# First query block of a hybrid encoder step: the products with x's low part put last, and a fixed VectorE order in the prologue

## The chip, the cores and the metric

The kernel runs on one core of a Trainium2 chip. The metric is the time of one execution in microseconds (us) on the device, as the median of several. Smaller is better. Engines are TensorE (PE; PEld its weight loads), VectorE (DVE), ScalarE (ACT), GpSimd (POOL) and SyncE (SP), whose queue issues all transfers.

## The reference

One inference step of a one-layer encoder. x (1024 prompt and 128 sample tokens, 1024 wide) is projected by one matrix into the queries, keys and values of three groups of heads and into a gate. The heads are band attention (A), differential attention (B) and attention to 256 memory tokens (M), whose keys and values are projected from `mem`.

```python
h = jnp.einsum('bsd,de->bse', x, w_in)
a_q, a_k, a_v, b_q, b_k, b_v, m_q, gate = jnp.split(h, PROJ_SPLITS, axis=-1)
mk, mv = memory_kv(mem_prompt, w_mem_kv[layer])
o_a = band_attention_prompt(aq, ak, av, a_rel_bias[layer])
o_b = diff_post(diff_attention_prompt(bq, bk, bv, lam), diff_subln_g[layer], lambda_init)
o_m = memory_attention(mq, mk, mv)
y = jnp.einsum('bse,ed->bsd', mixed * jax.nn.silu(gate), w_out)
return layer_norm(DEEPNORM_ALPHA * x + y, g, b)
```

## The kernel before

Every product is made of three passes over numbers that are split into a high part and a low part: high by high, low by high, high by low (`step`, L141 to L144). The high part is a cast on ScalarE into a shorter format; the low part is the number less its high part, a subtraction (`tensor_tensor`) with two inputs in SBUF, on VectorE or GpSimd.

**The prologue** (L192 to L278) does the following. `load_mem_w` (L202) loads and splits the weights of four memory blocks (two of keys, two of values) and, with block 0, `mem`; some subtractions are VectorE's, the rest GpSimd's. `load_next` (L129) loads and splits the weights of the next block of the projection; their low parts are GpSimd's. `load_x` (L222) loads a chunk c of x: x is cut into three chunks of 384 tokens (`CH`), each loaded in four pieces of two k-tiles, twelve pieces in all. ScalarE casts every piece (L199); the low parts (L200) of the odd pieces are VectorE's, those of the even pieces GpSimd's (`XP`). The pieces go through six buffers (`xr`), so that from the seventh on a piece's transfer waits until an earlier piece has been split. `mem_part` (L245) makes a memory block: 24 products of 256 columns (`mem_block`), a copy out of PSUM on VectorE (L236), and for the values (blocks 2 and 3) two transposes and a copy on ScalarE. `split_mem` (L178) splits the first unit's keys (`split_k`, L163: four casts on ScalarE, L167 and L168, two VectorE subtractions, L169) and its values (L183, L184). The tiles of the weights of blocks 2 and 3 (`ka`, `va`) are taken over by the split keys and values.

**The first query block** (L1117 to L1120) projects x into the queries of memory unit M0: for each chunk, `chunk` (L316) emits eight k-steps of the three passes, 24 products of 384 columns, and then `evac`: `split_q` (L147) takes the chunk out of PSUM in two halves, each a ScalarE activation (L155) and a VectorE subtraction (L159) with one input in PSUM. The products go into PSUM tiles `pp`, of which there are two; a chunk therefore waits until the chunk two places before it has been evacuated. Behind the query block come B0's keys (`k_block`) and the attention of M0, whose scores (L444, L445) need the split queries and keys.

**What sets the order.** A list scheduler places the instructions of each engine by priority and by its own estimate of when operands are ready; `manual_schedule(engines={...})` keeps the program's order for the engines named. Before, that held for SP in the prologue and for TensorE within one k-step. Each engine then runs its list strictly in order.

Of the kernel before, what the change touches and what calls it, by code (L numbers as in the profile page):

```python
# [7 lines left out]
F32 = mybir.dt.float32  # L8
# [7 lines left out]
P = 128  # L16
KT = 8
NTOK = 1152
NPR = 1024
CH = 384  # L20
# [2 lines left out]
EPS = 1e-5  # L23
BIG = 1e30
SP_ = 100
HP = 300
RR = 0.98
RL = 0.95
# [8 lines left out]
XP = [2, 6]  # L37
# [4 lines left out]
NG = [0, 1, 1, 1, 1, 1, 1, 2]  # L42
GW = 2
PE = mybir.EngineType.PE
SP = mybir.EngineType.SP
GATES = [2, 3, 4, 5, 0, 1, 6, 7]
SWAP = [i ^ 1 for i in range(32)]
# [15 lines left out]
def hybrid_step(tc, d, o):  # L63
    nc = tc.nc
# [11 lines left out]
    ps_p = pool("ps_p", 2, space=PSUM)  # L76
# [36 lines left out]
    names = [(n[0], int(n[1])) for n in ORD]  # L113
    base = {"A": (0, 2, 4), "B": (6, 10, 14), "M": (18,)}
    order = [base[names[0][0]][0] + names[0][1]]
    gates = iter(GATES)
# [5 lines left out]
    loaded = {}  # L122
# [6 lines left out]
    def load_next(early=None):  # L129
        if len(loaded) == len(order):  # L130
            return
        blk = order[len(loaded)]
        hi = wst.tile([P, KT, P], F32R, tag="whi")
        lo = wst.tile([P, KT, P], F32R, tag="wlo")
        loaded[blk] = (hi, lo)
        for i in range(2):
            raw = early.tile([P, 4, P], F32, tag="mraw", bufs=MB) if early else wst.tile([P, 4, P], F32, tag="wraw")
            nc.sync.dma_start(raw, d["win"][blk, :, 512 * i : 512 * i + 512].rearrange("p (k c) -> p k c", c=P))
            split_half(hi, lo, raw, i, nc.gpsimd)
# [32 lines left out]
    def setup(kind, idx):  # L172
        u = Unit()
        u.kind, u.idx = kind, idx
        u.slot = {"A": 0, "B": 2, "M": 6}[kind] + idx
        u.sqz = sqzs[ORD.index(kind + str(idx)) % 2]
        return u

    def split_mem(u, kv, v):
        u.ka = [op_.tile([P, 256], F32R, tag=f"ka{i}") for i in range(2)]  # L180
        split_k(kv, 256, u.ka, kl, 0)
        u.va = op_.tile([P, 2, 2, P], F32R, tag="va")
        nc.scalar.copy(u.va[:, :, :, 0:64], v)  # L183
        nc.vector.tensor_tensor(out=u.va[:, :, :, 64:128], in0=v, in1=f(u.va[:, :, :, 0:64]), op=ALU.subtract)  # L184
# [7 lines left out]
    with tc.tile_pool(name="early", bufs=1) as ep_:  # L192
        ep = Pool(ep_)
        memh = ep.tile([P, KT, 256], F32R, tag="memh")
        meml = ep.tile([P, KT, 256], F32R, tag="meml")
        wm = []

        def split_part(hi, lo, raw, a, b, eng):
            nc.scalar.copy(hi[:, a:b], raw)  # L199
            eng.tensor_tensor(out=lo[:, a:b], in0=raw, in1=f(hi[:, a:b]), op=ALU.subtract)  # L200

        def load_mem_w(blk):  # L202
            if blk < 2:
                hi, lo = [op_.tile([P, KT, P], F32R, tag=f"qa{i}", bufs=2) for i in range(2)]
            else:
                if blk == 2:
                    hi, lo = [op_.tile([P, KT, P], F32R, tag=f"ka{i}") for i in range(2)]
                else:
                    both = op_.tile([P, 2, KT, P], F32R, tag="va")
                    hi, lo = both[:, 0], both[:, 1]  # L210
            wm.append((hi, lo))
            cut = PC if blk == 0 else [0, 4, 8]
            for i, (a, b) in enumerate(zip(cut, cut[1:])):
                raw = ep.tile([P, b - a, P], F32, tag="mraw", bufs=MB)
                nc.sync.dma_start(raw, d["wmem"][blk, :, P * a : P * b].rearrange("p (k c) -> p k c", c=P))
                split_part(hi, lo, raw, a, b, nc.gpsimd if i or blk == 0 else nc.vector)
                if blk == 0:
                    memr = ep.tile([P, b - a, 256], F32, tag="xr", bufs=XB)
                    nc.sync.dma_start(memr, d["memT"][:, 256 * a : 256 * b].rearrange("p (k c) -> p k c", c=256))
                    split_part(memh, meml, memr, a, b, nc.vector)  # L220

        def load_x(c):  # L222
            for a in range(0, KT, 2):
                xr = ep.tile([P, 2, CH], F32, tag="xr", bufs=XB)
                nc.sync.dma_start(xr, d["xT"][c, :, CH * a : CH * (a + 2)].rearrange("p (k c) -> p k c", c=CH))
                split_part(xh[c], xl[c], xr, a, a + 2, nc.gpsimd if a in XP else nc.vector)

        kvs = []

        def mem_block(blk):  # L230
            ps = ps_p.tile([P, 256], F32, tag="pp")
            for k in range(KT):
                step(ps, wm[blk], memh, meml, k)
            kv = ep.tile([P, 256], F32, tag=f"memkv{blk}")
            kvs.append(kv)
            nc.vector.tensor_copy(kv, ps)  # L236


        warm = ps_t.tile([P, P], F32, tag="pt")
        for _ in range(WU):  # L240
            nc.tensor.matmul(warm, lhsT=sqzs[0][0], rhs=sqzs[0][0], start=True, stop=True)
        stores = []
        mem0 = []

        def mem_part(blk):  # L245
            mem_block(blk)
            out, scr = (o["mkT"], mkscr) if blk < 2 else (o["mvT"], mvscr)
            stores.append((out[blk % 2], kvs[blk]))
            if blk == 1:
                stores.append((mkscr, kvs[blk]))  # L250
            if blk < 2:
                return
            pt = ps_t.tile([P, 2, P], F32, tag="pt")
            for t in range(2):
                nc.tensor.transpose(pt[:, t], kvs[blk][:, t * P : (t + 1) * P], ident)
            mv = ep.tile([P, 2, P], F32, tag=f"memv{blk}")
            nc.scalar.copy(mv, pt)
            if blk == 3:
                stores.append((mvscr.rearrange("p (t e) -> p t e", t=2), mv))
            else:  # L260
                mem0.append(mv)

        with tc.manual_schedule(engines={SP}):
            for blk in range(4):
                load_mem_w(blk)
            load_next(ep)
            load_x(0)
            for blk in range(4):
                mem_part(blk)
            load_x(1)  # L270
            load_x(2)
            load_next()
            for out, kv in stores:
                nc.sync.dma_start(out, kv)
            nc.sync.dma_start(cos, d["cos"])
            nc.sync.dma_start(sin, d["sin"])
        units = [setup(*n) for n in names]
        split_mem(units[0], kvs[0], mem0[0].rearrange("p t (h e) -> p t h e", h=2))  # L278

    tmp = pool("tmp", 2)  # L280
    pp = pool("pp", 6)
# [56 lines left out]
    def project(blk, evac):  # L338
        return [chunk(blk, c, evac, c == 0) for c in range(3)]
# [9 lines left out]
        nc.vector.tensor_tensor(out=t1, in0=t1, in1=t2, op=ALU.add)  # L349
        return t1  # L350

    def q_block(u, blk, scale):
        def evac(c, ps):
            if c == 0:
                u.qa = [op_.tile([P, NPR], F32R, tag=f"qa{i}", bufs=2) for i in range(2)]
            n = npr(c)
            if u.kind == "B":
                src, sc = rope(ps, c, scale), 1.0
            else:
                src, sc = ps, scale  # L360
            split_q(src, sc, n, u.qa, c * CH)
            if c == 2:
                for m in range(2):
                    r = slice(64 * m, 64 * m + 64)
                    nc.scalar.activation(u.sqz[m][r], src[r, n:CH], AF.Copy, scale=sc)

        return project(blk, evac)

    def k_block(u, blk, out, skip):
        def evac(c, ps):  # L370
# [54 lines left out]
    def gate_block(slot):  # L425


        def evac(c, ps):
            t = tmp.tile([P, CH], F32, tag="t1", bufs=3)
            nc.scalar.activation(t, ps, AF.Tanh, scale=0.5)  # L430
            nc.vector.scalar_tensor_tensor(out=t, in0=t, scalar=1.0, in1=ps, op0=ALU.add, op1=ALU.mult)
            nc.sync.dma_start(
                gscr[3 * c : 3 * c + 3, :, slot].rearrange("t p c -> p t c"), t.rearrange("p (t c) -> p t c", c=P))

        return project(20 + slot, evac)
# [493 lines left out]
    def emit(items):  # L929
        for x in items:  # L930
            x[1]()
# [24 lines left out]
    def q_of(u):  # L956
        return q_block(u, base[u.kind][0] + u.idx, -0.125 if u.kind == "A" else 0.125)

    def k_of(u):
        if u.kind == "M":  # L960
            if u is not units[0]:
                load_mem(u)
            return []
        if u.kind == "B":
            return k_block(u, 10 + u.idx, o["bkT"][u.idx], 0)
        return k_block(u, 2 + u.idx, o["akT"][u.idx], 512)
# [147 lines left out]

    stages = []
    late = []
    first = [q_of(units[0])] + [gate_block(next(gates)) for _ in range(NG[0])]  # L1117
    for parts in zip(*first):
        for part in parts:
            emit(part)  # L1120
    for i, u in enumerate(units):
        nxt = units[i + 1] if i + 1 < len(units) else None
        emit(with_stages(sum(k_of(u), []), EV))
# [139 lines left out]
```

## Time and profile before

| what | value |
|---|---|
| runs | 685.92, 685.08, 683.6 us |
| median | 685.08 us |
| profiled execution | 685.8 us, its span 684.0 us |
| TensorE busy | 662.8 us (97%) |
| VectorE busy | 472.6 us (69%) |
| ScalarE busy | 356.3 us (52%) |
| GpSimd busy | 233.5 us (34%) |

The times of the profile count from the start of the span. A matmul's duration in the rows is its latency; matmuls overlap, so two in a row start closer together than they last. A row of the timeline merges equal neighbours (x2, x3) and ends, where the engine had been idle, with that idle time and what ended it.

### The profile page before, as it was taken

Reading aid. Unit: us, or ns where it says so; the run is one execution under the profiler, and the core shown is the slowest. Engines: PE = TensorE matmul, PEld = TensorE weight load, DVE = VectorE, ACT = ScalarE, POOL = GpSimd, SP = SyncE. Lnnn points to the kernel's source line nnn. Section 1 sums busy time; section 2 is a strip of 40 time slices with the busy share of each in tenths; the row PEclk is TensorE's granted clock in tenths of the full one; section 3 lists DMA queues with packets and bytes.
Section 4 is the critical chain, followed back from the end, with each engine's and each line's share of the span. In section 5 each row is a group of like instructions: output and inputs, shape, how many; then the busy total and the mean of one; then the engine's idle time right before and its main releaser. Section 6 shows DMA issues by size and latency. Waiting matters only on the chain. (4 is left out here: it accounts for less than half of the span.)

```text
span 684.0 us, 12210 instructions
## 1 busy us (share of the span) xinstructions
PE 662.8 (97%) x4306; PEld 614.2 (90%) x4306; DVE 472.6 (69%) x1169; ACT 356.3 (52%) x922; POOL 233.5 (34%) x282
## 2 busy tenths in 40 slices
PE   8899999999999999999999999999999996999995
PEld 7789999999999999999999999999999985787884
DVE  4869966796579856897566435673666678677854
ACT  5748845566446645565456535764566684111000
POOL 7654212632344224532323433323133231324102
PEclk9999999999999999999999999999999998899999
DMA  8761432121312222142302132233222648684411
GB/s 276 247 218 45 150 130 74 39 87 54 97 58 78 82 86 74 41 165 83 87 29 78 59 90 63 78 104 103 84 82 89 206 135 305 219 285 156 154 61 62
DMA packets 55694, 78.91 MB, mean 115 GB/s; under 512 B 9369, under 2 KB 33233, under 8 KB 55633
## 3 DMA queue, kind: packets, MB, share of 16 engines
q1 hardware_dynamic: 55632, 78.13, 34.6%
q8 instruction: 34, 0.56, 0.3%
q14 instruction: 28, 0.22, 0.1%
HBM read 57.69 MB, written 20.42 MB: 114 GB/s over the span
## 5 line engine op out<-in xcount | busy, mean ns | idle before, releaser
L143 PE MATMUL pp<-xl,whi 128*128 128x384 f32 x672 | 229.1, 341 | 2.6 <-DVE xl L200 1.8
L142 PE MATMUL pp<-xh,whi 128*128 128x384 f32 x672 | 230.5, 343 | 0.3 <-DVE qa L159 0.2
L144 PE MATMUL pp<-xh,wlo 128*128 128x384 f32 x672 | 228.9, 341 | 0.0
L143 PEld LDWEIGHTS pp<-xl,whi 128*128 128x128 f32 x672 | 126.6, 188 | 5.8 <-DVE xl L200 2.4
L142 PEld LDWEIGHTS pp<-xh,whi 128*128 128x128 f32 x672 | 126.4, 188 | 3.4 <-issue 0.7
L144 PEld LDWEIGHTS pp<-xh,wlo 128*128 128x128 f32 x672 | 126.4, 188 | 1.7 <-issue 0.2
L127 POOL TENSOR_TENSOR wlo<-wraw,whi 128x512 fp32r<-128x512 f32 x54 | 72.4, 1361 | 66.1 <-ACT whi L126 50.9
L586 ACT ACTIVATE p<-ps,nm 128x512 f32<-128x512 f32 (+3 forms) x96 | 55.2, 580 | 47.8 <-DVE nm L583 36.2
L444 PE MATMUL ps<-ka,qa 128*128 128x512 f32 (+4 forms) x176 | 58.5, 338 | 0.5 <-DVE nm L693 0.5
L445 PE MATMUL ps<-kl,qa 128*128 128x512 f32 (+4 forms) x176 | 57.3, 328 | 0.0
L457 PE MATMUL pt<-ident,p 128*128 128x128 f32 x332 | 55.0, 274 | 0.7 <-DVE p L526 0.6
L581 DVE TENSOR_REDUCE nm<-ps 128x1 f32<-128x512 f32 (+3 forms) x96 | 51.0, 549 | 1.6
L461 DVE TENSOR_TENSOR ptl<-pt,pth 128x512 fp32r<-128x512 f32 x56 | 38.2, 684 | 12.2 <-ACT pth L460 11.7
L457 PEld LDWEIGHTS pt<-ident,p 128*128 128x128 f32 x332 | 39.6, 141 | 4.4 <-DVE p L526 0.8
L701 POOL TENSOR_SCALAR p<-p,rs 128x640 f32<-128x640 f32 (+4 forms) x32 | 21.5, 676 | 64.3 <-DVE rs L700 58.7
L460 ACT CAST pth<-pt 128x512 fp32r<-128x512 f32 x56 | 32.6, 588 | 20.9 <-PE pt L457 19.9
L1028 PE MATMUL pp<-xh,whi 128*128 128x512 f32 (+1 forms) x96 | 37.5, 392 | 4.5 <-ACT whi L992 4.5
L1028 PE MATMUL pp<-xh,wlo 128*128 128x512 f32 (+1 forms) x96 | 37.0, 387 | 1.4 <-DVE rs L1051 1.4
L1028 PE MATMUL pp<-xl,whi 128*128 128x512 f32 (+1 forms) x96 | 37.1, 386 | 0.0
L992 ACT CAST whi<-p 128x1024 fp32r<-128x1024 f32 (+2 forms) x9 | 8.6, 954 | 53.5 <-PE pp L1028 42.9
L465 DVE TENSOR_TENSOR ptl<-pt,pth 128x256 fp32r<-128x256 f32 (+1 forms) x72 | 25.2, 352 | 15.8 <-ACT pth L464 15.2
L620 PE MATMUL po<-pth,va 128*128 128x256 f32 (+1 forms) x160 | 35.4, 285 | 0.0
(225 smaller groups left out, 1352.9 us busy)
## 6 DMA issues: line engine op xcount, KB each, us to landing
wraw<-in_win SPq DMA_DIRECT2D x54, 256.0 KB, 3.2
xr<-in_xT SPq DMA_DIRECT2D x12, 384.0 KB, 4.0
gates<-t SPq DMA_DIRECT2D x24, 192.0 KB, 2.2
qa<-in_xn SPq DMA_DIRECT2D x9, 512.0 KB, 5.0
wraw<-in_wout SPq DMA_DIRECT2D x16, 256.0 KB, 2.6
p<-gates SPq DMA_DIRECT2D x8, 512.0 KB
out_y<-qa SPq DMA_DIRECT2D x16, 256.0 KB, 2.3
mixed<-od SPq DMA_DIRECT2D x28, 128.0 KB, 1.8
```

The costliest lines, as they stand in the source:

```text
L127: eng.tensor_tensor(out=lo[:, h], in0=raw, in1=f(hi[:, h]), op=ALU.subtract)
L142: nc.tensor.matmul(ps, lhsT=w[0][:, k], rhs=xh_[:, k], start=(k == 0), stop=False)
L143: nc.tensor.matmul(ps, lhsT=w[0][:, k], rhs=xl_[:, k], start=False, stop=False)
L144: nc.tensor.matmul(ps, lhsT=w[1][:, k], rhs=xh_[:, k], start=False, stop=(k == KT - 1))
L444: nc.tensor.matmul(ps, lhsT=u.qa[h][:, qs], rhs=u.ka[h][:, k0 : k0 + n], start=True, stop=False)
L445: nc.tensor.matmul(ps, lhsT=u.qa[h][:, qs], rhs=kl[h][:, k0 : k0 + n], start=False, stop=True)
L457: nc.tensor.transpose(pt[:, t, q * P : (q + 1) * P], p[q][:, cols[t][q] : cols[t][q] + P], ident)
L461: nc.vector.tensor_tensor(out=lo, in0=pt, in1=f(hi), op=ALU.subtract)
L581: nc.vector.tensor_reduce(out=nm[:, m, c : c + 1], in_=ps[c][:, : b - a], axis=AX.X, op=ALU.max, negate=True)
L586: nc.scalar.activation(e[:, a:b], ps[c][:, : b - a], AF.Exp, bias=nm[:, m, 0:1], accum_out=rs[:, m, c : c + 1])
L620: nc.tensor.matmul(out, lhsT=a, rhs=b, start=(g == 0 and x == 0), stop=(g == j and x == len(mm) - 1))
L1028: nc.tensor.matmul(y, lhsT=a[:, k], rhs=b[k][:, s], start=(k == 0 and x == 0), stop=(k == KT - 1 and x == 2))
```

## The change

Three things are edited. First, `q_first` takes the place of the first query block's loop: for chunks 0 and 1, and then for chunk 2, it emits the 16 products with x's high part for each chunk, and after those the eight with x's low part, followed by the evacuation. Second, in the prologue VectorE is added to the engines that keep the program's order, and that program is written in another order: all weight splits, memory blocks 0 to 2, x's chunk 0, memory block 3, chunks 1 and 2, and only then `split_mem`. Third, the casts and subtractions of x get a higher priority (`XPR`).

```diff
@@ load_x
-                split_part(xh[c], xl[c], xr, a, a + 2, nc.gpsimd if a in XP else nc.vector)
+                with tc.high_priority(offset=XPR):
+                    split_part(xh[c], xl[c], xr, a, a + 2, nc.gpsimd if a in XP else nc.vector)
@@ prologue
-        with tc.manual_schedule(engines={SP}):
+        units = [setup(*n) for n in names]
+        with tc.manual_schedule(engines={SP, DVE}):
             for blk in range(4):
                 load_mem_w(blk)
             load_next(ep)
+            for blk in range(3):
+                mem_part(blk)
             load_x(0)
-            for blk in range(4):
-                mem_part(blk)
+            mem_part(3)
             load_x(1)
             load_x(2)
+            split_mem(units[0], kvs[0], mem0[0].rearrange("p t (h e) -> p t h e", h=2))
             load_next()
...
-        units = [setup(*n) for n in names]
-        split_mem(units[0], kvs[0], mem0[0].rearrange("p t (h e) -> p t h e", h=2))
@@ query block
+    def q_first(u):
+
+        evac = q_evac(u, 0.125)
+        blk = base[u.kind][0] + u.idx
+        for cs in ((0, 1), (2,)):
+            ps = {}
+            for low in range(2):
+                for c in cs:
+                    if not low:
+                        ps[c] = ps_p.tile([P, CH], F32, tag="pp")
+                        if c == 0:
+                            load_next()
+                    w = loaded[blk]
+                    with tc.manual_schedule(engines={PE}):
+                        for k in range(KT):
+                            if low:
+                                nc.tensor.matmul(ps[c], lhsT=w[0][:, k], rhs=xl[c][:, k], start=False, stop=(k == KT - 1))
+                            else:
+                                nc.tensor.matmul(ps[c], lhsT=w[0][:, k], rhs=xh[c][:, k], start=(k == 0), stop=False)
+                                nc.tensor.matmul(ps[c], lhsT=w[1][:, k], rhs=xh[c][:, k], start=False, stop=False)
+                    if low:
+                        with tc.high_priority(offset=HP):
+                            evac(c, ps[c])
...
-    first = [q_of(units[0])] + [gate_block(next(gates)) for _ in range(NG[0])]
-    for parts in zip(*first):
-        for part in parts:
-            emit(part)
+    q_first(units[0])
```

`q_evac` is the evacuation that `q_block` had, as a function of its own.

How VectorE's list reads where the memory part ends. Here `memkv` is the copy of a memory block, `qa`, `ka` and `va` on the left of L200 (L202) are low parts of memory weights. Before:

```order
L200 TENSOR_TENSOR qa_45_178<-mraw_179,qa_44_177 128x512
L236 COPY memkv_64_257<-pp_232 128x256
L200 TENSOR_TENSOR ka_49_188<-mraw_189,ka_48_187 128x512
L200 TENSOR_TENSOR va_197<-mraw_198,va_197 128x512
L299 TENSOR_SCALAR subg_92<-subg_92 128x1
L236 COPY memkv_66_284<-pp_259 128x256
```

Changed:

```order
L202 TENSOR_TENSOR qa_45_178<-mraw_179,qa_44_177 128x512
L202 TENSOR_TENSOR ka_49_188<-mraw_189,ka_48_187 128x512
L202 TENSOR_TENSOR va_197<-mraw_198,va_197 128x512
L239 COPY memkv_60_241<-pp_216 128x256
L303 TENSOR_SCALAR subg_92<-subg_92 128x1
L239 COPY memkv_62_268<-pp_243 128x256
```

The copy of block 0 moved behind the splits of the weights of blocks 2 and 3.

VectorE's list from there to the evacuation of chunk 1. `xl` is x's low part, `kl` that of the unit's keys, `va` on the left of L184 (L186) that of its values, `qa` on the left of L159 (L161) a half of the queries. Before, the key and value splits stand in the first five of these rows, ahead of x's chunks 1 and 2:

```order
L169 TENSOR_TENSOR kl_21_112<-memkv_64_257,ka_87_401 64x256
L169 TENSOR_TENSOR kl_22_113<-memkv_64_257,ka_88_402 64x256
L236 COPY memkv_72_343<-pp_318 128x256
L200 TENSOR_TENSOR xl_24_120<-xr_224,xh_23_119 128x768
L184 TENSOR_TENSOR va_409<-memv_70_316,va_409 128x4x64
L200 TENSOR_TENSOR xl_26_122<-xr_350,xh_25_121 128x768
L200 TENSOR_TENSOR xl_26_122<-xr_358,xh_25_121 128x768
L159 SCALAR_TENSOR_TENSOR qa_97_500<-pp_451,qa_97_500 64x384
L200 TENSOR_TENSOR xl_28_124<-xr_366,xh_27_123 128x768
L159 SCALAR_TENSOR_TENSOR qa_98_501<-pp_451,qa_98_501 64x384
L200 TENSOR_TENSOR xl_28_124<-xr_374,xh_27_123 128x768
L159 SCALAR_TENSOR_TENSOR qa_97_500<-pp_506,qa_97_500 64x384
```

Changed:

```order
L239 COPY memkv_72_343<-pp_318 128x256
L202 TENSOR_TENSOR xl_26_122<-xr_350,xh_25_121 128x768
L202 TENSOR_TENSOR xl_26_122<-xr_358,xh_25_121 128x768
L202 TENSOR_TENSOR xl_28_124<-xr_366,xh_27_123 128x768
L161 SCALAR_TENSOR_TENSOR qa_98_502<-pp_441,qa_98_502 64x384
L202 TENSOR_TENSOR xl_28_124<-xr_374,xh_27_123 128x768
L171 TENSOR_TENSOR kl_21_112<-memkv_60_241,ka_83_382 64x256
L171 TENSOR_TENSOR kl_22_113<-memkv_60_241,ka_84_383 64x256
L186 TENSOR_TENSOR va_390<-memv_66_300,va_390 128x4x64
L161 SCALAR_TENSOR_TENSOR qa_99_503<-pp_441,qa_99_503 64x384
L161 SCALAR_TENSOR_TENSOR qa_98_502<-pp_471,qa_98_502 64x384
L161 SCALAR_TENSOR_TENSOR qa_99_503<-pp_471,qa_99_503 64x384
```

The splits of the keys and values moved behind the last x split, and with them the second half of chunk 0's evacuation (`qa_99<-pp_441`), which now stands behind the values.

TensorE's list at the end of chunk 1 (`pp_471`, changed; chunk 0 is `pp_441`, chunk 2 `pp_523`), with the first scores `ps`:

```order
L982 MATMUL pp_471<-xl_26_122,whi_206 128x384 x8
L451 MATMUL ps_591<-ka_83_382,qa_98_502 128x256
L452 MATMUL ps_591<-kl_21_112,qa_98_502 128x256
L984 MATMUL pp_523<-xh_27_123,whi_206 128x384
L985 MATMUL pp_523<-xh_27_123,wlo_207 128x384
```

The eight products with x's low part stand at the end of the chunk; the first score pair stands between chunks 1 and 2, where before it stood within chunk 1.

## Rows read from the trace of the kernel before

**Rows 1.** The page: its first line, and TensorE's busy time.

```profile
span 684.0 us, 12210 instructions
...
PE 662.8 (97%) x4306; PEld 614.2 (90%) x4306; DVE 472.6 (69%) x1169; ACT 356.3 (52%) x922; POOL 233.5 (34%) x282
```

**Rows 2.** TensorE by stretches: stretch, length, busy (instructions), granted clock, DMA share, GB/s.

```profile
20.00:38.00 18.00, 15.21 (x85) 1.00 0.77 241
...
60.00:220.00 160.00, 159.91 (x1109) 1.00 0.27 84
```

**Rows 3.** TensorE's waits up to 60 us: total, times, longest.

```profile
PE pp L143 <- DVE xl L200: 1.8, 2, 1.6
```

**Rows 4.** Timeline of VectorE and GpSimd, 15 to 32 us: start, duration, instruction.

```profile
15.94 1.29 POOL L127 TENSOR_TENSOR wlo<-mraw,whi 128x512 fp32r<-128x512 f32 x1
...
19.23 0.86 DVE L169 TENSOR_TENSOR kl<-memkv,ka 64x256 fp32r<-64x256 f32 x2
...
22.41 2.57 POOL L200 TENSOR_TENSOR xl<-xr,xh 128x768 fp32r<-128x768 f32 x1
...
23.20 2.07 DVE L184 TENSOR_TENSOR va<-memv,va 128x256 fp32r<-128x256 f32 x1
...
24.93 2.02 POOL L200 TENSOR_TENSOR xl<-xr,xh 128x768 fp32r<-128x768 f32 x1
...
25.18 2.58 DVE L200 TENSOR_TENSOR xl<-xr,xh 128x768 fp32r<-128x768 f32 x1
...
30.89 0.96 DVE L200 TENSOR_TENSOR xl<-xr,xh 128x768 fp32r<-128x768 f32 x1
```

**Rows 5.** Timeline, 11 to 17 us: VectorE and TensorE in the memory part.

```profile
11.74 0.42 DVE L236 COPY memkv<-pp 128x256 f32<-128x256 f32 x1 [0.47 <-PE pp L144]
...
13.27 1.57 DVE L200 TENSOR_TENSOR va<-mraw,va 128x512 fp32r<-128x512 f32 x1
...
14.30 0.28 PE L144 MATMUL pp<-memh,qa 128*128 128x256 f32 x1
...
17.06 0.28 PE L142 MATMUL pp<-memh,va 128*128 128x256 f32 x1
```

**Rows 6.** Timeline of ScalarE, 18 to 20 us: first of four key casts; x's second piece.

```profile
18.00 0.40 ACT L167 CAST ka<-memkv 64x256 fp32r<-64x256 f32 x1
...
19.71 0.83 ACT L199 CAST xh<-xr 128x768 fp32r<-128x768 f32 x1
```

**Rows 7.** Timeline, 30 to 34 us: x's last piece, its transfer's issue and its cast.

```profile
30.30 0.33 SPq L225 DMA_DIRECT2D xr<-in_xT  x1
...
33.42 0.84 ACT L199 CAST xh<-xr 128x768 fp32r<-128x768 f32 x1
```

**Rows 8.** Timeline of TensorE, 28 to 30 us: two products of the block, ten steps apart.

```profile
28.09 0.34 PE L144 MATMUL pp<-xh,wlo 128*128 128x384 f32 x1
...
29.83 0.34 PE L142 MATMUL pp<-xh,whi 128*128 128x384 f32 x1
```

**Rows 9.** Timeline, 31 to 33 us: second half of chunk 0's evacuation; chunk 2's first product.

```profile
31.88 0.56 DVE L159 SCALAR_TENSOR_TENSOR qa<-pp,qa 64x384 fp32r<-64x384 f32 x1
...
32.58 0.41 PE L142 MATMUL pp<-xh,whi 128*128 128x384 f32 x1
```

**Rows 10.** TensorE, 577 to 586 us: timeline, then stretches as in rows 2.

```profile
577.26 0.79 PE L1028 MATMUL pp<-xh,whi 128*128 128x512 f32 x1 [4.54 <-ACT whi L992]
...
582.40 1.22 PE L1028 MATMUL pp<-xh,wlo 128*128 128x512 f32 x2 [1.36 <-DVE rs L1051]
...
577.00:578.00 1.00, 0.73 (x2) 0.50 0.92 317
...
585.00:586.00 1.00, 1.00 (x4) 0.69 0.94 362
```

**Rows 11.** Timeline of TensorE, 36 to 51 us: two later waits.

```profile
36.82 0.42 PE L142 MATMUL pp<-xh,whi 128*128 128x384 f32 x1 [0.22 <-DVE qa L159]
...
50.11 0.55 PE L457 MATMUL pt<-ident,p 128*128 128x128 f32 x3 [0.60 <-DVE p L526]
```

More of the change, by code (lines that the diff above doesn't have):

```diff
@@ L25 @@
 SP_ = 100
+XPR = 200
 HP = 300
@@ L44 @@
 PE = mybir.EngineType.PE
+DVE = mybir.EngineType.DVE
 SP = mybir.EngineType.SP
@@ L350, in rope, with q_evac @@
         return t1
-    def q_block(u, blk, scale):
+    def q_evac(u, scale):
         def evac(c, ps):
@@ L365, in evac, with q_block @@
                     nc.scalar.activation(u.sqz[m][r], src[r, n:CH], AF.Copy, scale=sc)
-        return project(blk, evac)
+        return evac
+    def q_block(u, blk, scale):
+        return project(blk, q_evac(u, scale))
     def k_block(u, blk, out, skip):
```

## Prediction

> **What bounds the kernel now.** I read the page first: TensorE is busy for 97% of the span [rows 1], so time can only come from its idle holes. The table of TensorE by stretches says where those are: 18.00 - 15.21 = 2.8 us of hole from 20 to 38 us, the stretch of the first query block [rows 2]; from 60 to 220 us it has 0.1 us in all. The waits name the larger part of the first hole: 1.8 us for x's low part from VectorE [rows 3]. That is what the edit goes after. Behind 60 us TensorE has no slack, so a delay or a gain up to there should reach the end in full.
>
> **How the port works.** The timeline of VectorE and GpSimd shows what makes the low parts late. A split of one x piece takes VectorE 0.96 us while GpSimd rests, but 2.58 us beside GpSimd: it begins at 25.18, GpSimd's split ends at 24.93 + 2.02 = 26.95, and VectorE's ends 0.81 later [rows 4]. The next-earlier pair is alike: the split of the values, a third of the size, begins at 23.20 and ends 0.29 after GpSimd's (24.98) [rows 4]. So two-input subtractions run in turns, each alone: 1.77 us for GpSimd (25.18 to 26.95), 0.81 for VectorE, and whoever waits goes next. Of the Trainium skill, "SBUF — State Buffer", section "SBUF: two separate sides", says that VectorE and GpSimd share a port pair under an exclusive lock, which a VectorE operation with two SBUF inputs takes against a GpSimd operation that reads SBUF; it adds that this is no split of bandwidth. By that rule the two key splits, of which no row here shows a blocked case, are held like the values' split and the sum below stands; with a mere slowing they would not be, and the sum would be that of the second rival.
>
> **The change, part by part.** No engine gets more or fewer operations; the edit reorders them, and SP's transfers keep their order up to the tables of cosines.
>
> *VectorE's fixed order in the memory part.* The copy of memory block 0 out of PSUM ran at 11.74, ahead of the last weight split (13.27 to 14.84) [rows 5]; now it stands behind it and ends at 14.84 + 0.4 = 15.2. Block 2 takes over that PSUM buffer and waits. TensorE's steps there are 0.12 apart: 17.06 - 14.30 = 2.76 us for 23 of them [rows 5]. Without the two early steps of block 2, block 1 is through at 14.2, so TensorE waits 1.05 us, and block 3 begins at 15.25 + 0.1 + 24 x 0.12 = 18.2 instead of 17.06.
>
> *Start of the x splits.* The key casts on ScalarE (0.43 apart, from 18.00 [rows 6]) overwrite block 2's weights and so wait for its end, now 18.3. Two of the four still stand ahead of the cast of x's second piece, which began at 19.71 [rows 6] and now begins at 18.3 + 0.86 = 19.15, ending near 20.0. From there GpSimd has work, and its six splits alternate with five of VectorE: 20.0 + 6 x 1.77 + 5 x 0.81 = 34.7 for the end of x's last piece. The loads keep up with this: the last one was issued at 30.30 and cast at 33.42 [rows 7], 3.1 later; it is now issued when VectorE's split of piece 7 ends (27.7), lands near 30.9, and is cast behind one evacuation by 32.2, where GpSimd wants it at 32.9.
>
> *TensorE's steps of the first block.* At 0.174 apart (1.74 us for ten [rows 8]) the 48 products of chunks 0 and 1 and two pairs of transposes take 8.9 us, from 21.1 to 30.0. By the turns above no low part is late for them (the last, from GpSimd, is there at 29.5). So the waits of [rows 3] do go: chunk 2, which began at 32.58 [rows 9], could follow chunk 1 and the score pair ahead of it (0.24) at 30.3, 2.3 us earlier.
>
> *What is late next.* Chunk 2 needs the PSUM buffer of chunk 0, which is free when both halves of the query have been subtracted out of it. In the new order of VectorE (second pair of order rows above) the second half stands behind the split of piece 11, both key splits and the values' split. The turns go on: VectorE's piece 11 ends at 32.9, GpSimd's piece 12 at 34.7, key split 0.43 [rows 4] to 35.1, GpSimd's next-weight split 1.29 [rows 4] to 36.4, key split to 36.8, the other weight split to 38.1, values' split 0.29 to 38.4, query half 0.56 [rows 9] to 38.95. Chunk 2 begins at 39.0; before, it began at 32.58, right behind that same half (31.88 + 0.56) [rows 9]. **+6.4 us.** TensorE has one score pair to do meanwhile, whose second product waits for the first key split itself. Bounds: 2.0 us if piece 12 comes too late to stand between (32.9 + 0.43 + 0.43 + 0.29 + 0.56 = 34.6); 7.0 if the x splits start half a microsecond later. I take 6.4, since every turn in [rows 4] went that way.
>
> *The clock.* Such a hole has one like it in the trace: after 4.54 us of waiting, TensorE resumes at 577.26 at a granted 0.50, the 1.2 GHz level, and is back at 2.4 GHz within the row from 585 [rows 10]. Less the second hole of 1.36 us [rows 10] that is 7 us of work at half rate, a loss of 3.5. A hole of 9 us with a single score pair in it must be expected to cost the same kind of thing; here no second hole follows, so between 0 and 3.5 I take **+2.0**. The Trainium skill, "TensorE: Matmul & The Clock Gate", Part 1, agrees that the slow level is the default and activity lifts it, but advises that for modelling the ramp is under 1% of a span and not to be fitted; left out on that advice, the sum would be 5.4. The row's 3.5 us are 0.5% of this span, so both hold.
>
> *Waits that go.* With TensorE this late, two later waits for VectorE find their results ready: 0.22 us at 36.82 and 0.60 at 50.11 [rows 11], with some 0.1 of restart each: **-1.0**. VectorE's softmax work behind it moves by less than TensorE's delay (the last transfer that it waits for is issued as soon as the early buffers are free, about when it was), so I add no new wait; that is an estimate.
>
> Sum: +6.4 + 2.0 - 1.0 = **+7.4 us**. Against the profiled execution (span 684.0 [rows 1], 1.8 around it, 685.8) that is 693.2; this execution stands 0.7 above the median of 685.08, so the forecast is **692.5 us**, about 1.1% slower. By the bounds the sum runs from 2.0 + 0 - 1.0 = +1.0 to 7.0 + 3.5 + 0 = +10.5.
>
> **Rivals.** *Faster: the waits go and nothing takes their place.* If VectorE kept the port whenever it has work, its pieces would follow their casts: piece 9 done near 27.9, piece 11 near 29.9, keys, values and query half by 31.6. Chunk 2 then begins 1.0 us earlier than before, and with the two waits gone the gain is 2.0; if chunk 2 followed directly on chunk 1 (30.0 plus a score pair), it is 2.3 + 1.0 = 3.3. I put it at **682.5**. It decides itself at whether the query's second half leaves chunk 0 before 32. The row at 25.18 speaks against it: VectorE's piece 5 was next on its engine at once, yet GpSimd went first [rows 4].
>
> *The same: the key and value splits slip through.* If piece 12 is cast after 32.9, or a small split isn't held, VectorE runs them in one go and chunk 2 begins at 34.6, with a hole too short or too broken to lower the clock: +2.0 - 1.0, or **686.1**. My margin there is 0.7 us.
>
> *The order is not what it says.* The listing puts six of chunk 0's eight low products ahead of chunk 1's high ones, so chunks are not really taken in pairs. This costs nothing by my count, as those low parts are there.
>
> **The numbers.** A measurement of this kernel tells about 0.3% (2.1 us) from no change. My forecast, with its smaller and larger variants, has 0.70; the faster rival 0.16; the same 0.14. The range runs from 685.0, the same-time rival with its +1.0 gone, to 696, which is the upper bound of +10.5 on the median; it leaves out the faster rival and a little at either end.
>
> **What would show it.** Right: TensorE idle from about 30 to 39 us but for one score pair, its wait naming VectorE's query half; a row for VectorE's values' split near 36 to 38 us that lasts over 1 us; a wait near 14.2 us on the copy of memory block 0; a granted clock of 0.50 in some rows after 34 us; from 220 us on the same order as before, shifted. Wrong: chunk 2 beginning before 34 us, or key splits of 0.4 us back to back while GpSimd works.

## The result and the profile after

| | before | changed |
|---|---|---|
| median | 685.5 us (683.6 to 685.99, 4 runs) | 693.68 us (691.0 to 694.62, 4 runs) |
| ratio, with its 95% interval | | 1.0111 (1.008 to 1.0141) |
| profiled execution, span | 684.0 us | 692.8 us |
| TensorE busy | 662.8 us | 667.6 us |

The kernel became 1.1% slower; 692.5 us was forecast. First the page of the changed kernel, against [rows 1]:

```profile
span 692.8 us, 12207 instructions
...
PE 667.6 (96%) x4306; PEld 620.0 (89%) x4306; DVE 474.7 (69%) x1169; ACT 356.3 (51%) x922; POOL 233.6 (34%) x282
```

TensorE has the same 4306 matmuls, yet is busy 4.8 us longer: some of them ran slower. The span is 8.8 us longer, so some 4 us are new holes. TensorE by stretches, against [rows 2]:

```profile
20.00:38.00 18.00, 11.66 (x69) 0.91 0.82 270
...
60.00:220.00 160.00, 159.44 (x1086) 1.00 0.25 80
```

The hole from 20 to 38 us grew from 2.8 to 18.00 - 11.66 = 6.3 us, and the granted clock is no longer 1.00 there (0.91). From 60 to 220 us TensorE is nearly as full as before (159.44 us against 159.91): what was lost earlier is not made good there. TensorE's waits up to 60 us, against [rows 3]:

```profile
PE ps L452 <- DVE kl L171: 3.5, 1, 3.5
PE pp L984 <- DVE qa L161: 2.9, 1, 2.9
...
PE ps L451 <- DVE qa L161: 0.8, 1, 0.8
```

The waits for x's low part are gone, as the edit meant. In their place stand 7.2 us of waits for a key split and for query halves, all on VectorE. The chain of waits from 30 to 40 us (start, duration, what; "issue" is time in which no wait shows) shows the queue that they stand in:

```profile
30.87 0.55 DVE qa L161
31.42 0.03 issue
31.45 1.87 DVE xl L202
33.32 1.94 DVE kl L171
35.27 0.03 issue
35.30 1.38 DVE kl L171
36.67 0.03 issue
36.71 1.37 DVE va L186
38.08 0.03 issue
38.11 0.57 DVE qa L161
38.68 0.14 issue
38.81 0.66 PE pp L984
```

Everything in it ahead of TensorE's product is one engine's list, in the order of the second changed fence of the section on the change. Two key splits of 0.43 us [rows 4] take 1.94 and 1.38, because GpSimd is at work all the while. Its timeline:

```profile
32.87 2.11 POOL L202 TENSOR_TENSOR xl<-xr,xh 128x768 fp32r<-128x768 f32 x1 [0.37 <-ACT xh L201]
34.95 2.85 POOL L129 TENSOR_TENSOR wlo<-wraw,whi 128x512 fp32r<-128x512 f32 x2
```

GpSimd's piece ends at 34.98 and VectorE's first key split 0.28 later (35.26); then a weight split, a key split, a weight split, and the value split: strict turns. Last, TensorE by stretches behind the hole:

```profile
34.00:36.00 2.00, 0.58 (x1) 0.67 0.91 271
36.00:38.00 2.00, 0.00 (x0) 0.50 0.92 334
...
42.00:44.00 2.00, 2.00 (x8) 0.50 0.64 250
44.00:46.00 2.00, 2.00 (x10) 0.77 0.00 0
46.00:48.00 2.00, 2.00 (x15) 1.00 0.01 4
```

The clock fell to 0.50 (1.2 GHz) in the hole and stayed there through nearly all of chunk 2. Its products start 0.32 us apart, where [rows 8] have 0.174:

```profile
40.23 0.52 PE L984 MATMUL pp<-xh,whi 128*128 128x384 f32 x1
40.55 0.52 PE L985 MATMUL pp<-xh,wlo 128*128 128x384 f32 x1
```

### The profile page after: what moved, and what is told of

Same layout as the page of the kernel before. It is cut to its first block, busy times and chain, and to the rows that moved or that the text cites. A ratio compares the mean times of both kernels' runs of the same rounds, so it can differ in the third digit from the quotient of the medians.

```text
span 692.8 us, 12207 instructions
## 1 busy us (share of the span) xinstructions
PE 667.6 (96%) x4306; PEld 620.0 (89%) x4306; DVE 474.7 (69%) x1169; ACT 356.3 (51%) x922; POOL 233.6 (34%) x282
## 4 chain that ended last, share of the span: by engine, by line
PE 82%; DMA 6%; DVE 5%; POOL 2%; ACT 2%; issue 2%; SPq 1%; POOLq 0%; DVEq 0%; ACTq 0%
PE pp L144 15%; PE pp L146 15%; PE pp L145 15%; PE pp L1059 7%; PE ps L1059 6%; PE pt L464 4%; PE ps L451 4%; PE ps L452 4%; PE po L627 4%; DMA wraw<-in_wout 3%; PE po L666 2%; PE pt L879 1%; POOL xl L1114 1%; PE ps L794 1%; DMA p<-gates 1%
## 5 line engine op out<-in xcount | busy, mean ns | idle before, releaser
L144 PE MATMUL pp<-xh,whi 128*128 128x384 f32 x648 | 222.2, 343 | 0.1
L145 PE MATMUL pp<-xl,whi 128*128 128x384 f32 x648 | 221.2, 341 | 0.0
L146 PE MATMUL pp<-xh,wlo 128*128 128x384 f32 x648 | 221.0, 341 | 0.0
L144 PEld LDWEIGHTS pp<-xh,whi 128*128 128x128 f32 x648 | 122.0, 188 | 2.9 <-DVE t L438 0.8
L145 PEld LDWEIGHTS pp<-xl,whi 128*128 128x128 f32 x648 | 122.0, 188 | 2.0
L146 PEld LDWEIGHTS pp<-xh,wlo 128*128 128x128 f32 x648 | 121.9, 188 | 2.0 <-issue 0.5
L468 DVE TENSOR_TENSOR ptl<-pt,pth 128x512 fp32r<-128x512 f32 x56 | 38.3, 685 | 11.1 <-ACT pth L467 10.6
L452 PEld LDWEIGHTS ps<-kl,qa 128*128 128x128 f32 x176 | 33.3, 189 | 3.9 <-DVE kl L171 3.7
L451 PEld LDWEIGHTS ps<-ka,qa 128*128 128x128 f32 x176 | 33.2, 189 | 2.5 <-DVE qa L161 1.1
```

The costliest lines, as they stand in the source:

```text
L144: nc.tensor.matmul(ps, lhsT=w[0][:, k], rhs=xh_[:, k], start=(k == 0), stop=False)
L145: nc.tensor.matmul(ps, lhsT=w[0][:, k], rhs=xl_[:, k], start=False, stop=False)
L146: nc.tensor.matmul(ps, lhsT=w[1][:, k], rhs=xh_[:, k], start=False, stop=(k == KT - 1))
L451: nc.tensor.matmul(ps, lhsT=u.qa[h][:, qs], rhs=u.ka[h][:, k0 : k0 + n], start=True, stop=False)
L452: nc.tensor.matmul(ps, lhsT=u.qa[h][:, qs], rhs=kl[h][:, k0 : k0 + n], start=False, stop=True)
L468: nc.vector.tensor_tensor(out=lo, in0=pt, in1=f(hi), op=ALU.subtract)
```

## Experiments

Theory A is the prediction's: chunk 2 waits for the PSUM buffer of chunk 0, whose second query half stands on VectorE behind three small splits, each held for a turn of GpSimd's. Theory B: the new block is late by its own form. Theory C: the clock, not the wait, is most of it. The scheduler answers an edit in one place with another order elsewhere, so most runs change one thing in one of the two kernels. Medians stand beside the ratio to the kernel before in the same comparison, with its 95% interval.

**The splits set back.** `split_mem` is called behind the fixed order, as before:

```diff
             load_x(2)
-            split_mem(units[0], kvs[0], ...)
             load_next()
...
             nc.sync.dma_start(sin, d["sin"])
+        split_mem(units[0], kvs[0], ...)
```

> The changed kernel with the call of split_mem set back behind the fixed order; VectorE's list then has the key splits behind x's first piece and the value split between two x pieces, and both query halves of chunk 0 with only one x split between them. Theory A (chunk 2 waits for the second query half, held on VectorE behind the key and value splits and GpSimd's turns): chunk 2 begins between 32.5 and 35.5 us instead of 38.81, no single hole of TensorE from 28 to 40 us over 4 us, time 684 to 688.5 us. Theory B (taking two chunks at a time is what makes chunk 0's buffer late, wherever the splits stand): chunk 2 stays within 1 us of 38.81, time 691 to 694. Theory C (most of the loss is TensorE's low clock, which comes by itself early in the kernel): time above 690 with chunk 2 before 36.

Measured: 688.52 us, 1.003 (1.0012 to 1.0048). VectorE, and TensorE's first product of chunk 2:

```profile
33.44 0.55 DVE L161 SCALAR_TENSOR_TENSOR qa<-pp,qa 64x384 fp32r<-64x384 f32 x1
34.02 0.96 DVE L202 TENSOR_TENSOR xl<-xr,xh 128x768 fp32r<-128x768 f32 x1
35.02 0.56 DVE L161 SCALAR_TENSOR_TENSOR qa<-pp,qa 64x384 fp32r<-64x384 f32 x1
```

```profile
35.72 0.66 PE L984 MATMUL pp<-xh,whi 128*128 128x384 f32 x1 [1.17 <-DVE qa L161]
```

Some 5 us came back by the move of three instructions that together last under 2 us when nothing holds them. B's 38.8 is refuted. A's price was a little low: chunk 2 began 0.2 us behind the expected stretch, the median lies just above its range, and the clock was at 0.50 here too, as the 0.66 us of that product show.

**The order alone.** The changed prologue, with the first block's loop as before:

```diff
-    q_first(units[0])
+    first = [q_of(units[0])] + [gate_block(next(gates)) for _ in range(NG[0])]
+    for parts in zip(*first):
+        for part in parts:
+            emit(part)
```

> The changed prologue and its fixed order of VectorE, with the first query block's loop as before (high and low products mixed, one chunk at a time). VectorE's list then has both query halves of chunk 0 ahead of the key and value splits. Theory A: the late splits alone don't hold chunk 2, which begins between 32 and 35 us; time 684 to 688.5. If late key splits cost by themselves, because the scores wait for them whatever the block does, TensorE shows a wait of over 2 us for the key split and the time is 689 or more. Theory B: about the time of before, 684 to 686.5.

Measured: 687.81 us, 1.0031 (1.0013 to 1.0049). Chunk 2 began at 31.17, ahead of the expected stretch, as both halves of chunk 0 stand ahead of the splits in this list. But chunk 1's halves don't, and so the wait sits one chunk later (TensorE):

```profile
36.40 0.39 PE L452 MATMUL ps<-kl,qa 128*128 128x256 f32 x1 [0.91 <-DVE kl L171]
39.61 0.41 PE L144 MATMUL pp<-xh,whi 128*128 128x384 f32 x1 [1.97 <-DVE qa L161]
```

The order costs by itself, some 2 us, and by the same mechanism.

**The block alone.** The kernel before with `q_first` and the priority of the x splits, its prologue untouched.

> The kernel before with the new first query block and the priority of the x splits, and nothing else: the prologue's program order and free VectorE of before. Theory A: the waits for x's low part are gone and nothing stands in their place, chunk 2 begins between 31 and 33.5 us, time 682 to 685. Theory B: chunk 2 begins at 36 us or later, time 690 or more. Theory C: in between, with a stretch of granted clock 0.50 between 6 and 20 us.

Measured: 683.29 us, 0.9961 (0.9948 to 0.9974): the block is a gain. Chunk 2 began at 33.69, 0.2 later than expected, since two waits are left on TensorE:

```profile
PE pp L981 <- DVE xl L202: 1.3, 1, 1.3
...
PE pp L983 <- DVE qa L161: 0.8, 1, 0.8
```

B falls for good. By the medians (685.98 us for the kernel before) one part gains 2.7 us and the other loses 1.8; together they lose 8 to 9. Most of the loss belongs to neither: only with both does chunk 0's second half stand behind the splits. Which share of the gain is the block's and which is the priority's was not tried apart.

**No x split on GpSimd**, in the changed kernel:

```diff
-XP = [2, 6]
+XP = []
```

> The changed kernel with all twelve x splits on VectorE and none on GpSimd. Theory A (VectorE and GpSimd take turns at two-input subtractions, 0.81 us for VectorE's and 1.77 for GpSimd's): every x split on VectorE takes 0.8 to 1.1 us, the last one ends by 34 us although VectorE has twice as many, chunk 2 begins between 31 and 34.5, time 682.5 to 687. Rival (VectorE's splits last long for a reason of their own, such as the transfers into the buffers): x splits stay above 1.5 us, the last ends after 37, chunk 2 begins at 38 us or later, time 691 or more.

Measured: 685.21 us, 0.9982 (0.9965 to 0.9999). VectorE's groups in the stretch of the x splits; first the changed kernel, then this one:

```profile
L202 DVE TENSOR_TENSOR xl<-xr,xh 128x768 fp32r<-128x768 f32 x6 | 10.7, 1800 | 2.5 <-ACT xh L201 2.4
```

```profile
L202 DVE TENSOR_TENSOR xl<-xr,xh 128x768 fp32r<-128x768 f32 x12 | 11.1, 954 | 1.8 <-ACT xh L201 1.6
```

Twelve splits alone keep VectorE busy as long as six beside GpSimd. Chunk 2 began at 30.95, at the early end of A's stretch. The fixed order still costs something here: chunk 1's halves stand behind the splits, and the next block's first product waits (TensorE):

```profile
38.32 0.41 PE L144 MATMUL pp<-xh,whi 128*128 128x384 f32 x1 [2.37 <-DVE qa L161]
```

That one instruction takes 954 ns alone and 1800 beside GpSimd would also fit two engines that slow each other down. That they take turns is shown by the chain above, where a key split ends 0.28 us behind GpSimd's piece. With this agrees the rule of the Trainium skill that the prediction drew on ("SBUF — State Buffer", section "SBUF: two separate sides": the pair is locked for a whole instruction).

**The changed kernel again**, unedited.

> The changed kernel once more, unedited, for more runs of it and a second trace. Theory A: again about 691 to 694.5 us, chunk 2 begins within 0.7 us of 38.8, and a stretch of granted clock 0.50 lies behind the hole at 31 to 39 us in this trace too. The other 0.50 stretch of the first trace, from 7 to 14 us, comes and goes from run to run, since the same instructions up to there ran at 1.00 in other kernels; if it belongs to the change it is there again.

Measured: 694.48 us, 1.0123 (1.0091 to 1.0154). Its trace has the wait at chunk 2 and one that the first trace did not show (TensorE):

```profile
15.17 0.36 PE L144 MATMUL pp<-memh,ka 128*128 128x256 f32 x1 [0.72 <-DVE subg L303]
```

```profile
38.22 0.66 PE L984 MATMUL pp<-xh,whi 128*128 128x384 f32 x1 [3.10 <-DVE qa L161]
```

The first is the wait for the copy of memory block 0, put down to the short instruction right behind that copy. The trace of the order alone has the same wait at 1.00 us. The early stretch of low clock was there again, but shorter.

**A spare buffer for chunk 2**, in the changed kernel:

```diff
-                        ps[c] = ps_p.tile([P, CH], F32, tag="pp")
+                        ps[c] = (ps_o if c == 2 else ps_p).tile([P, CH], F32, tag="po" if c == 2 else "pp")
```

> The changed kernel with chunk 2 of the first query block in a PSUM buffer of the attention outputs, which nothing else uses by then; VectorE's list keeps the second query half of chunk 0 behind the key and value splits. Theory A: chunk 2 no longer waits for that half, and most of it is done by 36 us; the wait for the half moves to the next block's first product, which takes chunk 0's buffer near 38 to 39 us instead of behind chunk 2 (45 us); time 685.5 to 690. Rival (chunk 2 is held by something else, such as x's last pieces or the score pair ahead of it): chunk 2 still begins after 37 us, time 691 or more.

Measured: 688.42 us, 1.0035 (1.0014 to 1.0055). TensorE works on chunk 2 from 29.42 on, in two pieces, and waits where A puts the wait, at the next block's first product:

```profile
37.23 0.42 PE L144 MATMUL pp<-xh,whi 128*128 128x384 f32 x1 [2.31 <-DVE qa L161]
```

VectorE's list has the same order here, so this shows that the PSUM buffer is the link by which the late half holds chunk 2. One thing differs on VectorE:

```profile
32.69 2.40 DVE L171 TENSOR_TENSOR kl<-memkv,ka 64x256 fp32r<-64x256 f32 x2
```

Here the key splits took 2.40 us, against 3.43 in the changed kernel's timeline: the first split began ahead of GpSimd's last x piece (32.69 against 32.83) and slipped through. GpSimd's line:

```profile
32.83 1.98 POOL L202 TENSOR_TENSOR xl<-xr,xh 128x768 fp32r<-128x768 f32 x1 [0.88 <-ACT xh L201]
```

That is the condition of the prediction's same-time rival, met by 0.14 us. But the second key split and the value split were held all the same, so the slip was worth 1.0 us and not the 4.4 (39.0 less 34.6) that the rival gave it.

**The clock by itself.** 48 further products between chunks 1 and 2, into a buffer that nobody reads:

```diff
+FILL = 48
...
+            if cs == (0, 1):
+                fill = ps_o.tile([P, CH], F32, tag="po")
+                with tc.manual_schedule(engines={PE}):
+                    for k in range(FILL):
+                        nc.tensor.matmul(fill, lhsT=loaded[blk][0][:, k % KT], rhs=xh[0][:, k % KT], start=True, stop=True)
```

> The changed kernel with 48 further products of 128x384 on TensorE between chunks 1 and 2, into a PSUM buffer that nobody reads, so that TensorE is busy while it waits for the query half. Theory A with the clock as a term of its own: chunk 2 still begins at 38 to 39.5 us, but the granted clock is 1.00 there and chunk 2's steps are 0.17 apart instead of 0.32; time 689 to 692, some 2 to 3 us under the changed kernel's. If the low clock costs nothing by itself (the steps behind the hole wait for other things anyway): time as the changed kernel's or above.

Measured: 690.01 us, 1.0076 (1.0051 to 1.01), 4.5 us under the changed kernel in the same comparison. TensorE:

```profile
31.93 6.40 PE L994 MATMUL po<-xh,whi 128*128 128x384 f32 x36
...
38.43 0.42 PE L985 MATMUL pp<-xh,whi 128*128 128x384 f32 x1
38.69 0.34 PE L986 MATMUL pp<-xh,wlo 128*128 128x384 f32 x1
...
38.00:40.00 2.00, 1.90 (x11) 1.00 0.43 73
```

Chunk 2 begins hardly earlier (38.43 against 38.81 and 38.22), but at full clock (1.00 in the last row, a stretch as above), and 8 us of useless work make the kernel faster. The gain is above the expected 2 to 3 us. The scheduler also moved the first score pairs behind chunk 2 in this kernel, so not all of it need be the clock.

**One call moved.** In the changed kernel, memory block 0's copy goes back ahead of two weight splits:

```diff
             for blk in range(4):
                 load_mem_w(blk)
+                if blk == 1:
+                    mem_part(0)
             load_next(ep)
-            for blk in range(3):
+            for blk in range(1, 3):
                 mem_part(blk)
```

> The changed kernel with one call moved: memory block 0's copy stands again ahead of the weight splits of blocks 2 and 3 in VectorE's fixed order. The scheduler then also puts both query halves of chunk 0 ahead of the key and value splits, while the halves of chunk 1 still stand behind them. Theory A: no wait near 14 us for the copy; chunk 2 begins between 31 and 34 us; the wait moves to the next block's first product, which needs chunk 1's buffer and begins at 38 to 39.5 us; time 685 to 688.5, some 6 us under the changed kernel's. Rival (the late key splits themselves hold TensorE): chunk 2's end or the scores wait for a key split by over 2 us, time 690 or more.

Measured: 683.73 us, 0.9964 (0.9949 to 0.9978). TensorE:

```profile
32.69 0.41 PE L986 MATMUL pp<-xh,whi 128*128 128x384 f32 x1 [0.88 <-DVE qa L161]
...
41.12 0.41 PE L144 MATMUL pp<-xh,whi 128*128 128x384 f32 x1 [2.47 <-DVE qa L161]
```

Chunk 2 and the place of the wait are as expected, but the second product comes 1.6 us behind the expected stretch, and the time is 1.3 us under its range. The rival is out: the longest wait for a key split is 0.69 us. This kernel's TensorE order differs from that of before over more than 400 us of the span, and in that long stretch its trace makes up more than it lost: 4.9 us late at 46 us of the kernel before, 0.9 early at the end. A shorter stretch of low clock near 580 us is part of that (3.3 us here, 10.2 before), but its length also differs between executions of one kernel: 10.1 and 3.4 us in the changed kernel's two traces. What in the later order does the rest was not tried and stays open.

**Versions without turns.** The new block on the old prologue with `XP = []`:

> The new first query block on the old prologue, with all x splits on VectorE. Theory A: both remaining waits of that block (1.3 us for x's low part, 0.8 for the query half) go or shrink below 0.6 us together, as no split has to take turns; chunk 2 begins between 30 and 32 us, time 680 to 683, below both kernels. If twelve splits are too many for VectorE alone, waits for x's low part above 1.5 us come back and the time is 684 or more.

Measured: 682.16 us, 0.9953 (0.9934 to 0.9972); no wait for a low part is left, and chunk 2 began at 31.91 behind 1.1 us for the query half, more than the 0.6 expected. The same with chunk 2 in the spare buffer:

> The new block on the old prologue, all x splits on VectorE, and chunk 2 in the PSUM buffer of the attention outputs. Theory A: the last wait for a query half (1.1 us) goes, time 679 to 682, about 1 us under the kernel without the spare buffer. If that wait only moves to the next block's first product, the same time as without it.

Measured: 682.99 us, 0.9946 (0.993 to 0.9962). The last wait is gone from the trace, yet the two intervals overlap almost wholly: no gain can be told. And the kernel before with `XP = []` and nothing else:

> The kernel before with all twelve x splits on VectorE, and nothing else. Theory A (turns with GpSimd are what made the low parts late): the waits of 1.6 and 0.8 us for x's low part shrink to under 0.5 us each, time 681 to 684 without the new block. If the order of the products was the cause, both waits stay and the time is 685 to 687.

Measured: 681.69 us, 0.993 (0.9914 to 0.9947), the lowest median of the study. TensorE from 20 to 38 us has no hole at all, against the 2.8 us of [rows 2]:

```profile
20.00:38.00 18.00, 18.00 (x114) 1.00 0.87 288
```

The low parts of [rows 3] were late because of the turns, and not because of the order of the products. The medians differ by 4.9 us, more than this hole; the wait of 0.60 us in [rows 11] is gone too, and the rest was not traced.

## Why the prediction was right

Each step follows the prediction's own.

*The memory part: right in the second trace, later and with another cause in the first.* Block 3 was to begin at 18.2 instead of 17.06, 1.1 late. In the first trace it began at 18.71, 1.65 late; in the second TensorE was 1.07 us late there. In the second the wait for the copy is named (0.72). In the first no such wait shows, because TensorE ran most of that stretch at a granted 0.50 and came too late to wait (the copy ended at 15.23, block 2 began at 15.83):

```profile
6.00:14.00 8.00, 7.45 (x32) 0.59 0.98 338
```

This stretch is not the change's doing: 8 of the 13 traces read for this study have one between 7 and 15 us, among them the four edited kernels that keep the old prologue; 5 have none, among them three with the changed prologue (the order alone, no x split on GpSimd, the filling products).

*The turns: right.* VectorE's piece 11 ended at 33.3, against 32.9. The two key splits and the values' split each waited for one turn. But it was closer than the prediction's margin of 0.7 us, since x's last piece was cast later than 32.2: GpSimd's last x piece began 0.45 us ahead of the end of VectorE's piece 11 (32.87 against 33.32) in the first trace and 0.15 in the second:

```profile
30.86 1.86 DVE L202 TENSOR_TENSOR xl<-xr,xh 128x768 fp32r<-128x768 f32 x1
```

```profile
32.57 1.81 POOL L202 TENSOR_TENSOR xl<-xr,xh 128x768 fp32r<-128x768 f32 x1 [0.66 <-ACT xh L201]
```

That the first key split was held at all was partly luck; with the spare buffer it was not.

*The low parts: right.* From 21.7 us to the end of chunk 1 at 30.70 (30.0 forecast) TensorE waits for none.

*What is late next: right.* Chunk 2 began at 38.81 (39.0 forecast), 6.2 us behind [rows 9] against +6.4. In the second trace it began at 38.22, 5.6 behind. The 0.6 between them is the same that block 3 was later in the first trace; that stretch of low clock was not forecast, so this much of the agreement is luck.

*The clock: right in kind, too small.* +2.0 was the estimate between 0 and 3.5. At half rate from 38.81 to about 44.9, TensorE took 7.06 us for chunk 2's 24 products, up to the next block's first at 45.87; at 0.174 apart they take 4.18, so it lost 2.9 us in the first trace. In the second the clock came back within 40 to 42 us and the loss was 1.7. The Trainium skill ("TensorE: Matmul & The Clock Gate", Part 1) says that for modelling the ramp costs under 1% of a typical span and that no particular count of slow matmuls should be fitted; by its number that holds, 2.9 of 692.8 us. But this is a third of the whole effect: left out, the sum would have missed by that much. The experiment with filling products moves it nearly by itself.

*The waits that go: right.* Neither of [rows 11] is in the trace. Before, TensorE's instructions ahead of these two waits started at

```profile
36.26 0.34 PE L142 MATMUL pp<-xh,whi 128*128 128x384 f32 x1
...
49.09 0.42 PE L143 MATMUL pp<-xl,whi 128*128 128x384 f32 x1
```

so the two steps took 0.56 and 1.02 us, where such steps take about 0.17 and 0.2 without a wait: -1.2 against -1.0.

*Behind that: left out.* TensorE's order differs between the two kernels from here on, so a matmul's place in the count tells the delay only where both have run the same set of products by then. At such places the delay is 8.6 us at 39 us of the kernel before, 6.6 at 84, 8.5 at 187 and 8.8 from 308 on. So the other order first gives back more than the second wait and later costs 1.9 us, of which one new wait is 0.48:

```profile
188.71 0.55 PE L464 MATMUL pt<-ident,p 128*128 128x128 f32 x3 [0.48 <-DVE rs L496]
```

The prediction put all this at nothing; on balance it costs 0.9 in this trace. The sum in the trace: 6.2 + 2.9 - 1.2 + 0.9 = +8.8, against +7.4. The low clock near 580 us has no part in it: it lasted 10.2 us before and 10.1 here.

The forecast of 692.5 is low by 1.2 us: 0.4 is the kernel before's own median in this comparison (685.5 against 685.08), and 0.8 is what the medians' difference of 8.2 has over the forecast's 7.4. In the traces the difference is 8.8, as the changed kernel's profiled execution (694.62 us) stands 0.9 above its median. Where the sum fell short are the clock's term and the one left out. Of the rivals, the faster one failed at its own condition: in the changed kernel's trace the two engines took strict turns, and chunk 0's second half left at 38.68, not before 32. The same-time rival came close at its condition, but its price was wrong: in the trace with the spare buffer one of the splits did slip through, and the two behind it were held none the less.

## What to carry to other kernels

When an engine is put on a fixed order, read in the new list which instruction that was not moved now stands behind the moved ones, and which buffer its consumer is waiting for: here an evacuation of 0.56 us behind three small splits held a whole chunk. Work given to a second engine that takes turns with the first was no relief here: compare the time that the first engine spends with and without it before splitting a job in two. Price a hole of several microseconds on TensorE with the clock that comes after it, not by its own length alone.

## What the runs showed that I had not expected

Six x splits on VectorE beside six on GpSimd keep VectorE busy for 10.7 us, all twelve for 11.1; so one constant in the old kernel is worth 0.7%, more than any reordering tried. Two edits that gain 0.4% and lose 0.3% alone lose 1.1 to 1.2% together. And TensorE finished earlier with 48 useless products than without them.
